# A two-layer encoder trunk on one core: where the modulated activations, their Winograd sums, the key transposes and two Fourier branch products stand

## The chip, the cores and the metric

The kernel runs on one core of a Trainium2 chip. The metric is the device time of one execution in microseconds, lower is better; the time of before is the median of three runs, 2324.62 us (2324.42 to 2328.24). Five engines matter: PE (TensorE, matrix products into PSUM), ACT (ScalarE), DVE (VectorE), POOL (GpSimd) and SP, whose queue here issues most DMAs. Each engine takes its own instructions in one fixed order.

## The reference, cut to what matters

Two groups of tokens (512 "sample" tokens and 256 "prompt" tokens, six tiles of 128 in all) pass the same DEPTH = 2 layers. What is computed per layer, with D = 1024:

```python
h = rms_norm(x, g_mix_pre) * (1 + sc1) + sh1
z = h @ w_in            # q latent 512 | kv latent 256 | rotary key 64 | Fourier input 512 | gates 2*1024
c_q, c_kv = rms_norm(z_q, g_q), rms_norm(z_kv, g_kv)
branch_a = attention(c_q @ w_q_b, c_kv @ w_kv_b, rotary parts) @ w_attn_o        # 8 heads
branch_b = fft2(u_f over sequence and 128 channels of a group).real @ w_four     # 4 groups
x = x + gt1 * rms_norm((sigmoid(gate_a) * branch_a + sigmoid(gate_b) * branch_b) @ w_out, g_mix_post)
h = rms_norm(x, g_ffn_pre) * (1 + sc2) + sh2
up = depthwise_conv3(h @ w_up)
x = x + gt2 * rms_norm((gelu(up_a) * up_b) @ w_down, g_ffn_post)
```

## The kernel before, in words

Every operand of a large product is kept as two rounded pieces, `hi` and `lo`, and a product is three matmuls: hi·hi, hi·lo, lo·hi. A piece pair costs one ACT copy (`hi`) and one DVE subtraction (`lo`); `split_from` (L195) does it from PSUM. Pools hold a fixed number of slots: 18 "doubles" (d, 128x1536), 21 "blocks" (w, 128x1024), 6 "rows" (r, 128x768), 8 PSUM banks (ps).

The work is a list of Steps. `run` walks it, and before each step it places the DMAs and the splits of weights that come due (by an estimate of PE time and the number of free blocks). The instructions of a step have a priority by their place in the list, which `tc.high_priority(offset=HP)` moves 50 forward. The framework then lays down one order for each engine: it plays the program through with its own estimates of durations and takes, whenever an engine is free, the ready instruction of the best priority, if it has a slot. On the chip that order is fixed; only waits move.

Per layer the list is, in the order of time:

- The join (end of the layer before): the last products of the feed-forward network (L1522 to L1524), per tile t the post step (L1579, L1582, mean squares on ACT L215), the residual (L684), the normalised rows (`pre_step`, L698), then h for each pair of tiles. POOL makes the reciprocal roots (L208, L211) and, at the join, the `lo` pieces of four weights (L162).
- h for a pair of tiles, the form of before at the join (`sums_h_step`): 16 transposes (L433), ACT writes a full-precision h block from PSUM (L436), ACT rounds it to `hi` (L441), DVE subtracts to `lo` (L442). For pair 1 the columns are also reversed (`reverse`, L717 on DVE and L718 on POOL). The form used for the last pair of the first layer (`h_step` with `to_h`, L374): transposes (L395), ACT writes `hi` from PSUM (L399), DVE computes `h*sc - hi` from PSUM into a row (L407) and then adds the shift, one half on DVE (L412), the other on ACT (L384), eight `hi` and eight `lo` columns a pair.
- The Fourier input products: `u_step(pair, i)`, four steps per pair of tiles and 12 matmuls a step (L802 to L804 in the second layer and for the first layer's pair 2, L1795 to L1797 for the first layer's pairs 0 and 1). `u_out` (L724 on) splits their result.
- `sums_step(pair)` (L447): four DVE additions hi + lo (L459) unless the full-precision block is at hand, four DVE differences (L471 to L477), and four splits (ACT L469, DVE L470). The result T is the moving operand of the gate products in Winograd form (`wino`, L607 to L609).
- Two plain gate products (`gate_step`, L190 to L193), 14 in Winograd form in seven `gate_pair`s, the Fourier transforms, then six key latents (`ckv_step`, L1007 to L1021, with a POOL root in each), six query latents (`cq_step`, L1034, L1036), their transposes (`kT`, `qT`, L1049 with ACT L1055 and DVE L1056), eight Fourier branch products (`four_step(m)`, 24 matmuls, two DVE multiplications L926 and L927, a POOL DMA that spills the row to DRAM, L928; the gate row comes in by an SP DMA, `load_sg`, L968), and two rotary steps (`qr`, 32 SP DMAs L1129).
- Attention (`attention`, L1148): keys and queries of a head (`k_step`, `qn_step`), rotary queries (`qr_split`, L1140), then units of scores (`sc_step`, L1229 to L1246: products, maximum, Exp, sum, scaling), transposes of the probabilities (`tr_step`, L1263) and products with V (`pv_step`).

`warm(func)` (L199) is one ACT instruction on a constant, made so that the table of `func` is loaded. Before, it stands at the end of the mixer (Exp) and of the attention (Gelu).

The order around the change:

```python
for b in range(2):
    o += [sums_step(b), gate_step(b, 7, spill(b))]
o.append(sums_step(2))
... ck[5:6], [kT(0)] + cq[0:1], [kT(1)] + cq[1:2], cq[2:3], cq[3:4], cq[4:5], [load_sg(0)] + cq[5:6],
fo[0], [qT(0)] + fo[1], [qT(1)] + fo[2], fo[3], [qr[0]] + fo[4], fo[5], [qr[1]] + fo[6], fo[7]
```

Of the kernel before, what the change touches and what calls it, by code (L numbers as in the profile page):

```python
# [48 lines left out]
def req_of(t):  # L49
    return 0 if t < 4 else 1  # L50
# [17 lines left out]
def encoder_trunk(ctx, tc, a, consts, y_prompt, y_sample):  # L68
# [29 lines left out]
    def blk(dt=F32, shape=(128, 1024)):  # L98
        blocks.append(wp.tile(list(shape), dt, tag="w", name=nm("w")))
        return blocks[-1]  # L100
# [9 lines left out]
    def bank():  # L110
        return pp.tile([128, 512], F32, tag="ps", name=nm("ps"))

    def f(ap):
        return ap.bitcast(F32)
# [81 lines left out]
        nc.scalar.activation(out=hi, in_=ps, func=AF.Copy)  # L196
        nc.vector.tensor_sub(out=lo, in0=ps, in1=f(hi))  # L197

    def warm(func):  # L199

        d = small(1)
        nc.scalar.activation(out=d, in_=neg_half, func=func)

    def rstd(sums, n=1):

# [206 lines left out]
                    nc.vector.tensor_scalar_add(out=lo[:, cols], in0=dd, scalar1=sh[:, k, r:r + 1])  # L412
        flush()

    def sums_h_step(sc, sh, pair, fold):

        r = req_of(2 * pair)

        def emit():
            if pair == 0:  # L420
                state["H"] = new_h()
            xns = [state.pop(("xn", 2 * pair)), state.pop(("xn", 2 * pair + 1))]
            c = slice(pair * 256, pair * 256 + 256)
            with tc.high_priority(offset=HP):
                h = [blk(F32, (128, 4, 2, 128)) for _ in range(2)]
                if pair == 2:
                    state["HR", pair] = h
                for i in range(4):
                    ps = bank()
                    for kk in range(2):  # L430
                        for j in range(2):
                            o = kk * 256 + j * 128
                            nc.tensor.transpose(ps[:, o:o + 128], xns[j](2 * i + kk), ident)  # L433
                    for kk in range(2):
                        k = 2 * i + kk
                        nc.scalar.activation(out=h[k // 4][:, k % 4].rearrange("p j c -> p (j c)"),  # L436
                                             in_=ps[:, kk * 256:kk * 256 + 256], func=AF.Identity,
                                             scale=state[sc][:, k, r:r + 1], bias=state[sh][:, k, r:r + 1])
                    z = h[i // 2][:, 2 * (i % 2):2 * (i % 2) + 2].rearrange("p k j c -> p k (j c)")
                    hi, lo = (x[:, :, c] for x in state["HD"][i])  # L440
                    nc.scalar.activation(out=hi, in_=z, func=AF.Copy)  # L441
                    nc.vector.tensor_sub(out=lo, in0=z, in1=f(hi))  # L442
                    if fold:
                        reverse(2 * i)
                        reverse(2 * i + 1)
        return Step(emit, 1.7)

    def sums_step(pair):

        def emit():  # L450
            if pair == 0:
                state["T"] = [(double(F32R, (128, 4, 384)), double(F32R, (128, 4, 384))) for _ in range(4)]
            h = state.pop(("HR", pair), None)
            if h is None:
                h = [blk(F32, (128, 4, 2, 128)) for _ in range(2)]
                for i in range(4):
                    hi, lo = (f(x[:, :, pair * 256:pair * 256 + 256]) for x in state["HD"][i])
                    z = h[i // 2][:, 2 * (i % 2):2 * (i % 2) + 2].rearrange("p k j c -> p k (j c)")
                    nc.vector.tensor_add(out=z, in0=hi, in1=lo)  # L459
            if pair == 2:  # L460
                del state["HD"]
            c = slice(pair * 128, pair * 128 + 128)
            r11, r12, r21, r22 = (h[kh][:, :, j, :] for kh in range(2) for j in range(2))
            t = [blk(F32, (128, 2, 4, 128)) for _ in range(2)]
            t1, t2, t3, t4 = t[0][:, 0], t[0][:, 1], t[1][:, 0], t[1][:, 1]

            def split(i, z):
                hi, lo = (x[:, :, c] for x in state["T"][i])
                nc.scalar.activation(out=hi, in_=z, func=AF.Copy)  # L469
                nc.vector.tensor_sub(out=lo, in0=z, in1=f(hi))  # L470
            nc.vector.tensor_sub(out=t1, in0=r12, in1=r11)  # L471
            split(0, t1)
            nc.vector.tensor_sub(out=t2, in0=r22, in1=t1)
            split(1, t2)
            nc.vector.tensor_sub(out=t3, in0=r22, in1=r12)
            split(2, t3)
            nc.vector.tensor_sub(out=t4, in0=r21, in1=t2)  # L477
            split(3, t4)
        return Step(emit, 0)
# [190 lines left out]
    def new_h():  # L670

        d = [(double(F32R), double(F32R)) for _ in range(4)]
        state["HD"] = [[z.rearrange("p (k c) -> p k c", k=2) for z in x] for x in d]
        return [tuple(z[:, k % 2, :] for z in state["HD"][k // 2]) for k in range(8)]
# [79 lines left out]
    def mixer_in(l, qr, fillers, start=None, tail=None):  # L754
# [54 lines left out]
            return Step(emit, 12 * 512 * MM_US, [uw[i]])  # L809

        us = [[u_step(p, i) for i in range(4)] for p in range(3)]
        out += start(uw, us, S) if start else []
        out += tail(us) if tail else []

# [148 lines left out]
        def late_mixer():  # L963

            def load_sg(m):
                def emit():
                    sgb[m] = row(F32)
                    nc.sync.dma_start(out=sgb[m], in_=gb_d[m])  # L968
                return Step(emit, 0)

            def spill(b):
                return lambda sg: nc.gpsimd.dma_start(out=(sig_d, gb_d)[b][7], in_=sg)
            o = []
            for b in range(2):
                o += [sums_step(b), gate_step(b, 7, spill(b))]
            o.append(sums_step(2))
            for m in range(7):
                st = gate_pair(m)
                if not m:
                    st = [st[i] for i in (0, 3, 1, 2, 4, 5, 6)]  # L980
                o += st[0:4] + (fill() if m else []) + st[4:]
            ck, cq = [ckv_step(t) for t in range(6)], [cq_step(t) for t in range(6)]
            fo = [[load_sg(m + 1) if m < 7 else Step(lambda: None, 0), four_step(m)] for m in range(8)]
            for x in ([dft[0], dft[1], ch[0]], [dft[2], ch[1], dft[3], ch[2]], ck[0:1], [ch[3]], ck[1:2], ck[2:3], ck[3:4],
                      ck[4:5], ck[5:6], [kT(0)] + cq[0:1], [kT(1)] + cq[1:2], cq[2:3], cq[3:4], cq[4:5], [load_sg(0)] + cq[5:6],
                      fo[0], [qT(0)] + fo[1], [qT(1)] + fo[2], fo[3], [qr[0]] + fo[4], fo[5], [qr[1]] + fo[6], fo[7]):
                o += x + fill()
            return o

# [71 lines left out]
        def kT(r):  # L1061
            def emit():
                lat_T(stage_k, 3, [vec["g_kv"][:, 0:1], vec["g_kv"][:, 1:2], None], kall, r)
                if r == 1:
                    stage_k.clear()
                    S["ckv", l], S["kr", l] = kall[0:2], kall[2]
            return Step(emit, 1.3)
# [10 lines left out]

        def end():
            S["H"] = None  # L1080
            warm(AF.Exp)
        out.append(Step(end, 0))
        return out

# [63 lines left out]
    def attention(l, qs, early):  # L1148
# [11 lines left out]
        def k_step(h):  # L1160
            w = kvw[h // 2]

            def emit():
                vh, vl = view(w, 2)
                c = slice((h % 2) * 256, (h % 2) * 256 + 128)
                p, q = bank(), bank()
                mm3_req((p, q[:, 0:256]), [(vh[:, k, c], vl[:, k, c]) for k in range(2)], S["ckv", l])
                if h % 2:
                    w.hi = w.lo = None
                hi, lo = pair()  # L1170
                split_from(p, hi[:, 0:512], lo[:, 0:512])
                split_from(q[:, 0:256], hi[:, 512:768], lo[:, 512:768])
                S["K", l][h] = (hi, lo)
            return Step(emit, 6 * 768 * MM_US, [w])

        def v_step(p, i):
# [155 lines left out]
        for u in range(n + 2):  # L1332
            if u < n:
                out.append(sc_step(u))
            if 0 <= u - 1 < n:
                out.append(tr_step(u - 1))
            out += fill[u]
            if 0 <= u - 2 < n:
                out.append(pv_step(u - 2))

        def end():
            S["ckv", l] = S["kr", l] = None
            warm(AF.Gelu_apprx_tanh)
        out.append(Step(end, 0))
        return out

# [105 lines left out]
    def ffn(l, h_last, fillers, last):  # L1452
# [203 lines left out]
                out += [ds[t] if t < NT - 1 else down_step(lc, [t], by_half=True), po[t], lo[t - 1]]  # L1656
            return out + [lo[NT - 1]]
        d45 = [down_step(lc, [4, 5], [j]) for j in range(starts[lc], NF)]
        h = [sums_h_step(("sc", l + 1, 1), ("sh", l + 1, 0), i, i == 1) for i in range(3)]
        out += [down_step(lc, [1], j1), po[1], ad[0], ad[1], pr[0], ds[2], po[2], pr[1], ad[2], ds[3], po[3], pr[2], ad[3]]  # L1660
        out += d45[0:1] + [pr[3]] + d45[1:2] + [h[0]] + d45[2:] + [po[4], po[5]]

# [249 lines left out]
```

## Time and profile before

| | before |
|---|---|
| median of 3 runs | 2324.62 us |
| the profiled execution | 2326.88 us, its span 2325.1 us |
| PE busy | 2267.4 us, 98% |
| DVE, ACT, POOL busy | 1669.4 us, 1314.4 us, 190.2 us |
| mean granted clock of PE | 0.984 |

Matmuls overlap, so a busy share counts an engine that has a matmul under way. A row of the waits says which instruction of which engine stood idle until which other one, for how long in total, how often, and the longest. A row of a timeline gives the start and duration, and in brackets the idle time of the engine just before it. A row of a stretch (A:B) gives its width, the busy time of each engine with the number of instructions, and the mean granted clock of PE, where 1.00 is the upper of its two levels, 2.4 GHz, and the other is half.

### The profile page before, as it was taken

The page shows a single profiled execution, that of the slowest core. Times are in us where ns is not written, and L with a number is a line of the kernel's source. Part 1 is how long each engine was busy: PE and PEld are TensorE (multiplying, and loading weights), DVE is VectorE, ACT ScalarE, POOL GpSimd, SP SyncE. Part 2 cuts the span into 40 slices and gives each one's busy share as a digit, 9 for nine tenths or more (in the row PEclk, how much of TensorE's full clock was granted, in tenths as well). Part 3 has the DMA queues.
Part 4 walks back from the last instruction along what each step waited for, and adds up shares of the span by engine and source line. Part 5 has one row for each costly group of instructions (what it writes and reads, how often), then busy time and mean ns, then how long its engine had stood idle before and what let it go on. Part 6 is the DMA issues. An engine that isn't in the chain of part 4 may idle for free. (4 is left out here: it accounts for less than half of the span.)

```text
span 2325.1 us, 33282 instructions
## 1 busy us (share of the span) xinstructions
PE 2267.4 (98%) x12582; PEld 2048.3 (88%) x12582; DVE 1669.4 (72%) x2712; ACT 1314.4 (57%) x2438; POOL 190.2 (8%) x317
## 2 busy tenths in 40 slices
PE   7999999999999999999989999999999999999998
PEld 5899788988899989999969988799888999999997
DVE  5976857765486887786868678677646886766677
ACT  4544516552466777777555543265425577777773
POOL 1001400000110000000130033000001000000001
PEclk9999999999989999999989999999999899999999
DMA  9356640133322433242333575302424232212223
GB/s 275 101 156 224 195 146 19 43 120 137 123 87 65 123 109 100 92 127 76 133 102 109 168 253 169 109 19 66 164 85 139 73 109 73 91 55 73 64 73 127
DMA packets 243805, 265.89 MB, mean 114 GB/s; under 512 B 20604, under 2 KB 193318, under 8 KB 243645
## 3 DMA queue, kind: packets, MB, share of 16 engines
q1 hardware_dynamic: 235885, 235.85, 32.8%
q0 software_dynamic: 7760, 27.92, 3.6%
q8 instruction: 99, 1.62, 0.3%
q14 instruction: 61, 0.50, 0.1%
HBM read 225.89 MB, written 31.54 MB: 111 GB/s over the span
## 5 line engine op out<-in xcount | busy, mean ns | idle before, releaser
L607 PE MATMUL ps<-d,w 128*128 128x384 f32 (+2 forms) x1680 | 565.2, 337 | 8.9 <-ACT ps L633 4.0
L608 PE MATMUL ps<-d,w 128*128 128x384 f32 (+2 forms) x1680 | 564.1, 336 | 0.6 <-DVE d L470 0.5
L609 PE MATMUL ps<-d,w 128*128 128x384 f32 (+2 forms) x1680 | 562.5, 335 | 0.0
L554 DVE TENSOR_TENSOR w<-w,w 128x512 fp32r<-128x512 f32 x406 | 271.6, 685 | 104.6 <-ACT w L553 101.9
L607 PEld LDWEIGHTS ps<-d,w 128*128 128x128 f32 x1680 | 322.7, 192 | 25.0 <-ACT ps L633 5.4
L608 PEld LDWEIGHTS ps<-d,w 128*128 128x128 f32 x1680 | 323.1, 192 | 10.7 <-DVE d L470 1.3
L609 PEld LDWEIGHTS ps<-d,w 128*128 128x128 f32 x1680 | 322.9, 192 | 0.9 <-DVE w L554 0.8
L553 ACT ACTIVATE w<-w 128x512 fp32r<-128x512 f32 x406 | 248.2, 626 | 71.5 <-PE ps L609 28.0
L190 PE MATMUL ps<-d,w 128*128 128x512 f32 x704 | 242.3, 345 | 0.0
L191 PE MATMUL ps<-d,w 128*128 128x512 f32 x704 | 222.2, 338 | 0.0
L161 ACT ACTIVATE w<-w 128x1024 fp32r<-128x1024 f32 (+4 forms) x140 | 141.1, 1015 | 91.9 <-PE ps L191 30.9
L319 DVE SCALAR_TENSOR_TENSOR w<-w,c,w 128x1024 f32<-128x1024 f32 x140 | 175.5, 1277 | 12.6 <-DMA w<-in_w_ada_dram 12.3
L162 DVE TENSOR_TENSOR w<-w,w 128x1024 fp32r<-128x1024 f32 (+3 forms) x136 | 157.6, 1167 | 35.7 <-ACT w L161 19.3
L193 PE MATMUL ps<-d,w 128*128 128x512 f32 x704 | 181.4, 339 | 0.0
L1560 ACT ACTIVATE w<-ps 128x512 f32<-128x512 f32 x216 | 127.4, 590 | 86.3 <-PE ps L1558 85.1
L1558 PE MATMUL ps<-w,d 128*128 128x512 f32 x432 | 171.3, 397 | 0.0
L1557 PE MATMUL ps<-w,d 128*128 128x512 f32 x432 | 170.5, 395 | 0.0
L1555 PE MATMUL ps<-w,d 128*128 128x512 f32 x432 | 167.6, 389 | 0.0
L190 PEld LDWEIGHTS ps<-d,w 128*128 128x128 f32 x704 | 132.8, 189 | 31.3 <-DVE r L926 1.7
L191 PEld LDWEIGHTS ps<-d,w 128*128 128x128 f32 x704 | 132.9, 189 | 16.2 <-DVE d L197 0.6
L1468 DVE SCALAR_TENSOR_TENSOR r<-r,v,r 128x511 f32<-128x511 f32 (+1 forms) x176 | 100.6, 613 | 33.9 <-ACT r L1465 33.6
L668 DVE TENSOR_TENSOR r<-ps,r 128x384 f32<-128x384 f32 (+2 forms) x92 | 49.3, 537 | 104.7 <-PE ps L609 104.6
(275 smaller groups left out, 4447.4 us busy)
## 6 DMA issues: line engine op xcount, KB each, us to landing
w<-in_w_up_dram SPq DMA_DIRECT2D x88, 512.0 KB, 3.9
w<-in_w_ada_dram SPq DMA_DIRECT2D x80, 512.0 KB, 3.7
w<-in_w_in_dram SPq DMA_DIRECT2D x48, 512.0 KB, 6.1
w<-in_w_down_dram SPq DMA_DIRECT2D x72, 256.0 KB, 2.9
xs<-w SPq DMA_DIRECT2D x18, 512.0 KB, 2.7
w<-xs SPq DMA_DIRECT2D x18, 512.0 KB, 3.8
w<-in_w_ada_dram SPq DMA_DIRECT2D x32, 256.0 KB, 5.8
w<-in_w_attn_o_dram SPq DMA_DIRECT2D x16, 512.0 KB, 3.6
```

The costliest lines, as they stand in the source:

```text
L190: nc.tensor.matmul(o, lh, rh[:, c0:c0 + s], start=(first and k == 0), stop=False)
L191: nc.tensor.matmul(o, lh, rl[:, c0:c0 + s], start=False, stop=False)
L193: nc.tensor.matmul(o, ll, rh[:, c0:c0 + s], start=False, stop=(last and k == n - 1))
L319: nc.vector.scalar_tensor_tensor(out=box[r], in0=x, scalar=c, in1=box[r], op0=ALU.mult, op1=ALU.add)
L553: nc.scalar.activation(out=us[i].hi, in_=z, func=AF.Copy)
L554: nc.vector.tensor_sub(out=us[i].lo, in0=z, in1=f(us[i].hi))
L607: nc.tensor.matmul(ps, wh[:, k], x, start=(start and k == 0), stop=False, skip_group_check=True)
L608: nc.tensor.matmul(ps, wh[:, k], y, start=False, stop=False, skip_group_check=True)
L609: nc.tensor.matmul(ps, wl[:, k], x, start=False, stop=(k == 3), skip_group_check=True)
L1555: nc.tensor.matmul(ps, gh[:, cc], dc.hi[:, o], start=(c == 0 and j == js[0]), stop=False, skip_group_check=True)
L1557: nc.tensor.matmul(ps, gh[:, cc], dc.lo[:, o], start=False, stop=False, skip_group_check=True)
L1558: nc.tensor.matmul(ps, gl[:, cc], dc.hi[:, o], start=False, stop=(j == js[-1]), skip_group_check=True)
```

## The change: what it does

Six edits, in both layers where not said otherwise:

1. At the join (second layer) h is made by `h_step`, the form that writes `hi` from PSUM. For pairs 0 and 1 it has the same priority as before; for pair 2 it has none. The full-precision block of pair 2 is no longer kept.
2. `sums_step(0)` stands before the last Fourier input product of pair 2, `sums_step(1)` behind it, `sums_step(2)` ahead of both plain gate products; before, each of the first two had a gate product behind it, and the third came after them.
3. `kT(0)` stands two, `kT(1)` three query latents later, `qT(0)` and `qT(1)` one Fourier product later.
4. The second rotary step stands one Fourier product earlier, and `four_step(6)` and `four_step(7)` with their `load_sg` stand in the attention, behind the score products of units 0 and 1.
5. The Exp warm-up reads a column of the first head's keys, and so follows them; it is issued in `k_step(0)`.
6. The Gelu warm-up reads a column of the last head's output.

```diff
+        us[2] = us[2][0:3] + [sums[0]] + us[2][3:] + [sums[1]]
...
-            o = []
-            for b in range(2):
-                o += [sums_step(b), gate_step(b, 7, spill(b))]
-            o.append(sums_step(2))
+            o = [sums[2]] + [gate_step(b, 7, spill(b)) for b in range(2)]
...
+            S["fo", l] = fo[6:8]
...
-                      ck[4:5], ck[5:6], [kT(0)] + cq[0:1], [kT(1)] + cq[1:2], cq[2:3], cq[3:4], cq[4:5], [load_sg(0)] + cq[5:6],
-                      fo[0], [qT(0)] + fo[1], [qT(1)] + fo[2], fo[3], [qr[0]] + fo[4], fo[5], [qr[1]] + fo[6], fo[7]):
+                      ck[4:5], ck[5:6], cq[0:1], cq[1:2], [kT(0)] + cq[2:3], cq[3:4], [kT(1)] + cq[4:5],
+                      [load_sg(0)] + cq[5:6], fo[0], fo[1], [qT(0)] + fo[2], [qT(1)] + fo[3], [qr[0]] + fo[4],
+                      [qr[1]] + fo[5]):
...
-            warm(AF.Exp)
...
+                if h == 0:
+                    warm(AF.Exp, hi[:, 0:1])
...
                 out.append(sc_step(u))
+            if u < 2:
+                out += S["fo", l][u]
...
-            warm(AF.Gelu_apprx_tanh)
+            warm(AF.Gelu_apprx_tanh, S["AT", l][NH - 1][0][:, 0:1])
...
-        h = [sums_h_step(("sc", l + 1, 1), ("sh", l + 1, 0), i, i == 1) for i in range(3)]
+        h = [h_step(("sc", l + 1, 1), ("sh", l + 1, 0), i, i == 1) for i in range(3)]
```

`sums_h_step` is removed, and `sums_step` always makes its four additions.

## Rows read from the trace of the kernel before

**Rows 1.** The page's first part: busy time, share of the span, instructions.
```profile
PE 2267.4 (98%) x12582; PEld 2048.3 (88%) x12582; DVE 1669.4 (72%) x2712; ACT 1314.4 (57%) x2438; POOL 190.2 (8%) x317
```

**Rows 2.** The waits of PE over the whole span: total us, times, longest us.
```profile
PE ps L1263 <- DVE w L1246: 8.9, 2, 4.5
PE ps L802 <- ACT d L441: 8.5, 2, 5.1
...
PE ps L179 <- DVE d L1020: 3.9, 2, 2.0
...
PE ps L607 <- ACT d L469: 3.0, 1, 3.0
...
PE ps L804 <- DVE d L442: 1.4, 1, 1.4
...
PE ps L433 <- DVE w L1579: 1.4, 1, 1.4
```

**Rows 3.** Six stretches: width, busy PE, PEld, DVE, ACT, POOL, granted clock, DMA.
```profile
88.00:108.00 20.00, 15.95 (x80) 14.66 (x79) 19.75 (x33) 11.39 (x22) 0.55 (x1) 0.91 0.34 99
236.00:262.00 26.00, 23.07 (x105) 17.27 (x104) 22.16 (x35) 10.30 (x21) 10.71 (x13) 0.93 0.58 191
340.00:366.00 26.00, 21.33 (x130) 18.67 (x130) 16.02 (x30) 13.76 (x29) 0.00 (x0) 0.93 0.25 69
1162.00:1230.00 68.00, 56.76 (x252) 45.24 (x251) 42.56 (x69) 36.27 (x76) 21.72 (x34) 0.90 0.30 93
1385.00:1411.00 26.00, 23.08 (x106) 17.31 (x105) 22.16 (x35) 10.30 (x21) 10.69 (x13) 0.93 0.60 194
1490.00:1516.00 26.00, 21.32 (x126) 18.62 (x126) 15.60 (x29) 13.73 (x28) 0.00 (x0) 0.87 0.21 59
```

**Rows 4.** Groups of DVE instructions, 62 to 108 us: busy us, mean ns, idle before.
```profile
L470 DVE TENSOR_TENSOR d<-w,d 128x512 fp32r<-128x512 f32 x12 | 7.9, 682 | 0.0
L459 DVE TENSOR_TENSOR w<-d,d 128x512 f32<-128x512 f32 x12 | 7.6, 681 | 0.0
...
L197 DVE TENSOR_TENSOR w<-ps,w 128x512 fp32r<-128x512 f32 x2 | 1.4, 686 | 2.2 <-ACT w L196 2.2
```

**Rows 5.** The stretch of one Fourier branch product, columns as in rows 3.
```profile
330.20:334.42 4.22, 4.22 (x27) 3.68 (x25) 2.19 (x4) 0.80 (x1) 0.70 (x2) 1.00 0.85 231
```

**Rows 6.** Timeline at the first attention's start: ACT table load, then DVE scaling.
```profile
350.79 1.28 ACT L1242 ACT_TABLE_LOAD   x1
...
354.23 0.87 DVE L1246 TENSOR_SCALAR w<-w,s 128x512 f32<-128x512 f32 x2
```

**Rows 7.** Rotary copies (ACT group, whole span), early warm-up (ACT), SP's rotary DMAs.
```profile
L1140 ACT ACTIVATE r<-d 128x768 fp32r<-128x768 f32 x16 | 13.5, 846 | 49.3 <-DMA d<-w 28.9 <-DMA mb_d<-r 18.0 <-PE ps L1233 2.4
...
281.57 1.28 ACT L202 ACT_TABLE_LOAD   x1
...
309.71 30.49 SPq L1129 DMA_DIRECT2D d<-w  x32
```

**Rows 8.** Timeline at the join: ACT, then DVE, then POOL.
```profile
1176.24 1.02 ACT L436 ACTIVATE w<-ps,m,m 128x256 f32<-128x256 f32 x2 [0.91 <-POOL w L162]
...
1210.07 1.06 ACT L749 ACTIVATE w<-w 128x1024 fp32r<-128x1024 f32 x1 [10.74 <-DVE w L746]
...
1159.42 0.87 DVE L698 TENSOR_SCALAR d<-w,s 128x512 f32<-128x512 f32 x2
...
1177.28 2.57 DVE L698 TENSOR_SCALAR d<-w,s 128x512 f32<-128x512 f32 x1 [4.56 <-ACT w L436]
...
1177.21 2.36 POOL L162 TENSOR_TENSOR w<-w,w 128x1024 fp32r<-128x1024 f32 x1
```

**Rows 9.** Groups of the first layer's pair 2, 54 to 63 us: ACT, DVE.
```profile
L399 ACT ACTIVATE d<-ps,m,m 128x256 fp32r<-128x256 f32 x8 | 3.9, 554 | 0.0
...
L407 DVE SCALAR_TENSOR_TENSOR r<-ps,m,d 128x256 f32<-128x256 f32 x8 | 3.7, 478 | 0.3 <-ACT d L399 0.3
L412 DVE TENSOR_SCALAR d<-r,m 128x256 fp32r<-128x256 f32 x4 | 1.4, 354 | 0.1
```

More of the change, by code (lines that the diff above doesn't have):

```diff
@@ L197, in split_from, with warm @@
         nc.vector.tensor_sub(out=lo, in0=ps, in1=f(hi))
-    def warm(func):
+    def warm(func, src=None):
         d = small(1)
-        nc.scalar.activation(out=d, in_=neg_half, func=func)
+        if src is None:
+            nc.scalar.activation(out=d, in_=neg_half, func=func)
+        else:
+            nc.scalar.activation(out=d, in_=f(src), func=func, scale=0.0)
     def rstd(sums, n=1):
@@ L413, in to_h @@
         flush()
[L415 to L446, printed above, removed]
     def sums_step(pair):
@@ L452, in emit @@
                 state["T"] = [(double(F32R, (128, 4, 384)), double(F32R, (128, 4, 384))) for _ in range(4)]
[L453 to L459, printed above, removed]
+            h = [blk(F32, (128, 4, 2, 128)) for _ in range(2)]
+            for i in range(4):
+                hi, lo = (f(x[:, :, pair * 256:pair * 256 + 256]) for x in state["HD"][i])
+                z = h[i // 2][:, 2 * (i % 2):2 * (i % 2) + 2].rearrange("p k j c -> p k (j c)")
+                nc.vector.tensor_add(out=z, in0=hi, in1=lo)
             if pair == 2:
@@ L811, in mixer_in @@
         us = [[u_step(p, i) for i in range(4)] for p in range(3)]
+        sums = [sums_step(i) for i in range(3)]
+        us[2] = us[2][0:3] + [sums[0]] + us[2][3:] + [sums[1]]
         out += start(uw, us, S) if start else []
```

## The prediction

> **What bounds the kernel now.** I read the busy times first: PE is busy 98% of the span, the next engine 72% [rows 1]. So time can come only from stretches in which PE stands still or runs at its lower clock, and an edit that takes work off another engine is worth nothing by itself. The second view is the list of PE's waits [rows 2]; the reader is to see how short it is, and that nearly all of it lies in six places: the sums of the first layer (L607, 3.0 us), the key transposes in both layers (L179, 3.9 us), the first transposes of probabilities in both layers (L1263, 8.9 us) and the join (L802, L804, L433: 8.5 + 1.4 + 1.4 us). The third view gives each place a stretch of its own, with PE's idle time and the granted clock [rows 3]. A wait is followed by a stay at 1.2 GHz, where the products take twice as long, so a place loses its idle time plus its busy time times (1 - clock):
>
> sums, first layer: 4.05 + 15.95 x 0.09 = 5.5 us; key transposes: 2.93 + 23.07 x 0.07 = 4.5 and, in the second layer, 4.5; attention's start: 4.67 + 21.33 x 0.07 = 6.2 and 4.68 + 21.32 x 0.13 = 7.5; join: 11.24 + 56.76 x 0.10 = 16.9. In all 45.1 us.
>
> The edits leave PE's products as they are, so 45.1 us is also about the most that they can gain. The question is what share of it comes back.
>
> **The change, part by part.**
>
> *The sums (edit 2).* A sums step is 12 DVE instructions of 128x512 at 0.68 us, some 0.6 us from start to start, and 4 ACT copies: 7.3 us of DVE, 22 us for three. In the first layer DVE is the late one there: 19.75 of 20 us busy while PE waits, with 2.2 us of idle time ahead of the first sums [rows 3, 4]. The move lets the first sums fill these 2.2 us, and puts the third ahead of the weight pieces (L554) that are made for later gate products; by an estimate six of these, at 0.68 us each as every instruction of this shape, stand ahead of the wait and can come after it. Together that is 2.2 + 4.1 us against a wait of 3.0 and its clock. Bounds: 0 (the weight pieces then are late instead) and 5.5. I take 4.0, since DVE has little to spare. In the second layer no wait of PE stands at the sums, so nothing is gained: 0. Cover for both: the last input product and two plain gate products, in which PE needs no sum.
>
> *Key transposes (edit 3).* In the key latents ACT stands on POOL's roots, the transposes then wait, and their PSUM banks hold up the next query latent; the wait is put down to L1020, one of the last DVE instructions of a key latent [rows 2]. With two and three query latents between, the chain is done when the transposes come. Nothing reads the keys before attention; the three tiles of key latents are only held longer. Bounds for a layer: 0 (the banks merely run out later, behind the same DVE work) and 4.5. I take 3.8, so 7.6 for both. The query transposes then have one Fourier product of 4.2 us [rows 5] ahead of the rotary step as cover, in place of two; if that is too short, a wait of a microsecond takes its place, which is in the 0.7 left.
>
> *Fourier products in attention, and the Exp table (edits 4 and 5).* At the start of attention PE has two score products and one key product, and then waits 4.5 us in each layer for the scaled probabilities (L1246). On the way lie a table load of 1.28 us and copies ahead of it on ACT [rows 2, 6]. The Exp warm-up of before had loaded at 281.57, 70 us early [rows 7]; the Gelu one behind it replaced the table, and the load fell into the chain. Two products of 4.2 us each [rows 5] now lie between the first scores and these transposes: 8.4 us of cover for 4.5, and either one nearly covers it alone; with the early table the chain is shorter by 1.28 besides. The new warm-up waits for a copy that stands ahead of it on ACT anyway; behind it stands the first query's copy, which comes only after a product as long as the two here. The products bring four DVE multiplications, 2.2 us [rows 5], on an engine with 16.0 of 26 us busy [rows 3], two spills by POOL, behind which nothing waits, and one SP load. SP is occupied by the rotary copies for 30.5 us up to 340.2 [rows 7]; the last of them are issued 4.2 us earlier now, as the second rotary step is, so the load is there in time. Bounds: 0 and 13.7. I take 12.5.
>
> *The Gelu warm-up (edit 6).* It takes a load away that no wait of PE stands behind: 0; the end of attention bears one load of 1.28 us on ACT, where PE has other products.
>
> *h at the join (edit 1).* For pair 0 ACT started at 1176.24, when POOL's weight piece had let go a block [rows 8]. The new form needs no block, so ACT can start when the transposes are done, before the last down products end, and the waits of 3.4 (8.5 - 5.1) and 1.4 us go. But pair 1 stays as late as it was: its last row is scaled from 1177.28 on and takes 2.57 us instead of the 0.4 of its like, beside a POOL weight piece of 2.36 us [rows 8]; its transposes stand in PE's fixed order among the products of pair 0, so I put 2 us of waiting there. For pair 2 ACT stood 10.7 us before a copy of `u_out` (L749), with h of pair 2 behind it [rows 8], and PE waited 5.1 us. Without its priority the transposes now come after the products of pair 1: ACT takes `hi` at once, but `lo` stands behind four DVE additions of `u_out` (2.7 us), so 2.6 us stay. The bank wait of 1.4 stays too. Price: a pair costs DVE 8 x 0.478 + 4 x 0.354 = 5.2 us [rows 9] against 4 x 0.68 = 2.7 before; three pairs and the additions that pair 2 now needs (2.7) make 10.2 us more, in a stretch with 25 idle DVE us of 68 [rows 3]. Left over: 2.0 + 2.6 + 1.4, and 2.5 for two stays at the lower clock, together 8.5. Gain 16.9 - 8.5 = 8.4. Bounds: -5 (half of the 10.2 us exposed) and 16.9.
>
> The row that speaks against this price is that 2.57: a DVE instruction from SBUF alone was held for as long as POOL's piece ran [rows 8]. By the Trainium skill ("SBUF — State Buffer", section "SBUF: two separate sides") VectorE and GpSimd take a shared port pair in turn, each for a whole instruction, and a VectorE operation in the two-port mode is shut out until GpSimd's ends. By that rule, with which the row agrees, `to_h`'s additions from SBUF (L412) could each wait a whole piece, 2.4 us, beside POOL's last two, and the join would give 3.6 instead of 8.4, 2297 in all.
>
> **Sum.** 4.0 + 7.6 + 12.5 + 8.4 = 32.5 us. From the profiled execution's own 2326.9 that gives 2294.4; the median of the runs shown is 2.3 us below it, so I predict 2292.
>
> **The rivals.**
>
> *The join gives nothing.* Pair 1's rows come no earlier, and PE's queue holds transposes that wait for them; beside POOL's last two pieces two of the additions L412 take 2.57 us instead of 0.35 (4.4 us), and 4 of DVE's 10.2 us more stand open. For it: all behind 1177 us hangs on a DVE instruction beside POOL [rows 8]. Against: pair 0 was late for a block alone, and pair 2 for an ACT order that ends. 2292 + 8.4 = 2300.
>
> *ACT stands on a row in attention.* The rotary copies (L1140) waited 18.0 us for spills of Fourier products, about 9 us in each layer [rows 7], as six rows are all. The last two spills now come later, and the first Exps may stand behind such a copy. Then the transposes come 8.9 - 1.3 us later, against 8.4 us of cover for what was a wait of 4.5: 3.7 us and 1.5 at the lower clock stay in each layer, and the 12.5 shrinks to 3.3: 2301.
>
> *The change doesn't do what it says.* The orders are laid down by estimates; they can put the transposes ahead of the products and the additions behind the weight pieces, as the Exp warm-up came 70 us early [rows 7]. All places keep their waits: 2324.
>
> *Slower: the products of the join lose their overlap.* If DVE works off the early sums (14.6 us for two) ahead of a pair's `lo`, each pair's h stands bare before its products: three times some 7 us by ACT's and DVE's rows [rows 9], 21 us, and between such waits all 144 products stay at 1.2 GHz, 512 x 144 columns at 4.22 us for 9,216 [rows 5], so 33.8 us more. The join loses 54.8 instead of 16.9, the rest gains 24.1: 2324.6 + 37.9 - 24.1 = 2338. It decides from a loss of 41 us at the join. Against: h of pairs 0 and 1 has priority, and a clock below 0.90 over 68 us is in no row.
>
> **How the numbers follow.** The forecast's case, 2284 to 2299, gets 0.55; the join without gain 0.18; the rows in attention 0.13; no effect 0.06; slower 0.08. The runs can tell 0.2% (4.6 us) from no change. Faster by more than that: the first three, 0.86. Within: 0.06. Slower: 0.08. The range goes from 2278, just under the 2279.5 at which all 45.1 us come back, to 2315, where each place gives little (1 + 2 + 6 + 0 us). It leaves out the last two cases, 0.14.
>
> **What would show it.** Right: L607 without a wait for L469 near 95 us; no L179 wait for L1020; no L1263 wait above 1 us, an ACT table load behind the first key copies and two warm loads fewer a layer; products of pair 0 right behind the last down products at the join, waits of 2 to 3 us for pairs 1 and 2. Wrong: PE waits on L926's banks or on L1140 in attention, L609's weights late at the first gate pair, a granted clock below 0.90 at the join, or a wait of over 5 us before pair 1 there.

## The result, and the profile after

The changed kernel takes 2294.65 us (median of 4 runs, 2293.9 to 2299.15) where the kernel before takes 2326.43 (4 runs beside it): a ratio of 0.9867, 95% interval 0.985 to 0.9885. Its profiled execution took 2294.44 us with a span of 2292.6, so the spans differ by 32.5 us; the sum of the prediction was 32.5. The time forecast was 2292: it took 2.3 us off because the three runs of before then known had their median below the profiled one, and with the fourth that median is 2326.43.

Where they come from is read best from the starts of PE's products, since both kernels do the same products. *Start* ends at the first input product (L802, now L770). A goes from the first gate pair of the first layer to its first Fourier transform, B from there to the last transposes of probabilities. C goes from the first down unit of the first layer to the first gate pair of the second, so it holds the join. D and E are A and B of the second layer. In us, worked out from the traces:

```
         start      A       B       C       D       E
before   61.24  110.39  309.32  544.18  105.09  309.80
after    59.85  106.92  299.88  537.13  104.37  299.84
gain      1.39    3.47    9.44    7.05    0.72    9.96
e1                              544.40  103.38
e2                      304.10                  304.15
e3              110.93                  112.78
e4                      304.07                  303.85
e5                      300.96                  301.25
e6                              535.31
e7                              527.87
e8                              532.98
e9                              532.98
e10                     302.67                  303.52
e11                     306.25                  305.85
e12             111.76          537.24          309.60
```

The experiments' rows (below) show only the stages that they bear on. Each row comes from one profiled execution. Where a stage has no edit, B and E differ by about 0.4 us at most between runs, C by 0.7, D by 1.2, A by up to 1.4 (before against e12). *Start* went from 59.23 to 62.40 over all runs with no edit in it, so its 1.4 us are not the change's; the experiments are compared by their stages first, by their medians second; the two differ by 3.4 us at most (e10).

The waits of PE after, over the whole span (total us, times, longest), to be held against [rows 2]:

```profile
PE ps L770 <- DVE r L410: 5.0, 1, 5.0
PE ps L575 <- ACT ps L601: 4.5, 6, 1.1
...
PE ps L180 <- DVE w L162: 2.0, 2, 1.0
PE ps L398 <- DVE w L1551: 1.4, 1, 1.4
```

The waits of the sums, of L179 and of L1263 (now L1233) are gone; the second row was there before with 4.0 us. One long wait is new: five microseconds at the join, behind an instruction that the prediction does not name. The stretches that answer to [rows 3], with the same columns, each aligned to the same work:

```profile
86.00:106.00 20.00, 18.57 (x103) 17.16 (x102) 18.72 (x32) 12.91 (x25) 1.09 (x2) 1.00 0.35 99
236.00:262.00 26.00, 24.99 (x122) 19.71 (x121) 24.18 (x32) 11.07 (x22) 6.65 (x10) 1.00 0.75 214
328.00:354.00 26.00, 25.11 (x153) 21.66 (x152) 20.97 (x37) 14.93 (x31) 1.17 (x2) 1.00 0.29 94
1145.00:1213.00 68.00, 60.97 (x288) 49.97 (x287) 57.94 (x110) 39.39 (x82) 27.63 (x36) 0.95 0.33 105
1370.00:1396.00 26.00, 24.99 (x120) 19.65 (x119) 24.09 (x32) 10.62 (x22) 6.73 (x10) 1.00 0.64 191
1458.00:1484.00 26.00, 25.11 (x153) 21.68 (x152) 20.07 (x35) 13.67 (x30) 1.18 (x2) 1.00 0.34 107
```

Five of the six now run at 1.00 throughout, with about 1 us of idle time each. The join keeps 7.03 us of idle time and a clock of 0.95: 7.03 + 60.97 x 0.05 = 10.1 us of its 16.9 are still lost. DVE, POOL, ACT and PE there (start, duration, in brackets the idle time before; in this order):

```profile
1146.07 3.59 DVE L652 SCALAR_TENSOR_TENSOR w<-d,s,w 128x512 f32<-128x512 f32 x2 [0.45 <-POOL s L214]
...
1152.90 3.06 DVE L666 TENSOR_SCALAR d<-w,s 128x512 f32<-128x512 f32 x2 [0.84 <-POOL s L214]
...
1162.41 2.55 DVE L666 TENSOR_SCALAR d<-w,s 128x512 f32<-128x512 f32 x1 [3.55 <-POOL s L214]
1164.89 0.86 DVE L410 SCALAR_TENSOR_TENSOR r<-ps,m,d 128x256 f32<-128x256 f32 x2
...
1146.05 2.40 POOL L162 TENSOR_TENSOR w<-w,w 128x1024 fp32r<-128x1024 f32 x1
...
1152.83 2.39 POOL L162 TENSOR_TENSOR w<-w,w 128x1024 fp32r<-128x1024 f32 x1
...
1158.94 2.40 POOL L162 TENSOR_TENSOR w<-w,w 128x1024 fp32r<-128x1024 f32 x1 [2.57 <-PE ps L1496]
1161.44 0.30 POOL L211 TENSOR_SCALAR s<-s 128x1 f32<-128x1 f32 x1
...
1162.35 2.34 POOL L162 TENSOR_TENSOR w<-w,w 128x1024 fp32r<-128x1024 f32 x1
...
1159.74 0.19 ACT L218 ACTIVATION_READ_ACCUMULATOR d<-w 128x1 f32 x1
...
1165.90 0.77 PE L770 MATMUL ps<-w,d 128*128 128x512 f32 x1 [4.99 <-DVE r L410]
1167.34 2.79 PE L398 MATMUL ps<-ident,d 128*128 128x128 f32 x12 [0.67 <-DVE r L410]
```

Pair 0's products start at 1160.07, right behind the last down products, and stop after three of them: the fourth waits 5.0 us, and pair 1's transposes (L398) behind it another 0.7. The fourth waits for L410, whose output no product reads: so it must be waiting for a PSUM bank of pair 0's transposes, which L410 has still to read. L410 stands behind L666 of row 3 in DVE's order; L666 waits 3.55 us for POOL's root, which stands behind a weight piece (row 3's mean square on ACT ends at 1159.93, the root L211 starts at 1161.44, so 1.5 us of it); and then L666 runs beside the next piece and takes 2.55 us. That is the reading; e6 to e9 test it. (Line numbers differ a little from kernel to kernel.)

### The profile page after: what moved, and what is told of

Same layout as the page of the kernel before. It is cut to its first block, busy times and chain, and to the rows that moved or that the text cites. A ratio compares the mean times of both kernels' runs of the same rounds, so it can differ in the third digit from the quotient of the medians.

```text
span 2292.6 us, 33289 instructions
## 1 busy us (share of the span) xinstructions
PE 2252.8 (98%) x12582; PEld 2037.7 (89%) x12582; DVE 1676.0 (73%) x2740; ACT 1306.9 (57%) x2434; POOL 187.4 (8%) x317
## 5 line engine op out<-in xcount | busy, mean ns | idle before, releaser
L162 DVE TENSOR_TENSOR w<-w,w 128x1024 fp32r<-128x1024 f32 (+3 forms) x136 | 158.0, 1168 | 31.7 <-ACT w L161 15.1
```

## The experiments

**Undoing one part.** *e1*: `h = [sums_h_step(...)]` at the join in place of `h_step`, with the kept block.

> The changed kernel, but with h at the join made as before: ACT writes a full-precision block, then hi and lo come from it, with priority for all three pairs, and the third sums step uses the kept block. The other five edits stay. Theory A (each edit has its own stretch, and the gains add): the stretch from the first product of the final down projection to the first gate pair of the second layer is 7.0 us longer, 2301.7 in all; PE waits again for h of pair 0 (3 to 5 us) and of pair 2. Theory B (the join got faster because the sums of the second layer moved, not because of the new h): no more than 2 us, 2296.5. Theory C (the early sums take DVE from the old h of pair 2, which the priority does not prevent for instructions already under way): more than 9 us, 2304 or above.

2300.57 us (0.9889, 0.9876 to 0.9903). C is 544.40, 7.27 longer than after and as long as before, with the waits of before:

```profile
PE ps L805 <- ACT d L444: 8.5, 2, 5.1
PE ps L807 <- DVE d L445: 1.4, 1, 1.4
```

Theory A for the place and the size: with the sums where the change puts them, the old h brings back the whole loss. That h alone was the cause does not follow (e7).

*e2*:
```diff
-cq[0:1], cq[1:2], [kT(0)] + cq[2:3], cq[3:4], [kT(1)] + cq[4:5],
+[kT(0)] + cq[0:1], [kT(1)] + cq[1:2], cq[2:3], cq[3:4], cq[4:5],
```

> The changed kernel, but with the two key transposes behind the first and second query latent as before; the query transposes and all else as changed. Theory A (the transposes waited for the chain of the last key latent, and two query latents are enough cover): the waits of L179 for the key chain come back, 3.5 us in each layer with the stay at the lower clock, 2301.7. Theory B (the banks run out behind the same DVE work wherever the transposes stand): within 2 us of the changed kernel.

2300.23 us (0.9889, 0.9876 to 0.9903); B and E are 4.2 and 4.3 longer, and the wait of [rows 2] is back to the tenth of a microsecond. Theory A. By medians the loss is 5.6 us and not 8.5: the profiled execution, 2302.5 us, was the longest of the four.

```profile
PE ps L179 <- DVE d L989: 3.9, 2, 2.0
```

*e3*:
```diff
-us[2] = us[2][0:3] + [sums[0]] + us[2][3:] + [sums[1]]
-o = [sums[2]] + [gate_step(b, 7, spill(b)) for b in range(2)]
+o = [sums[0], gate_step(0, 7, spill(0)), sums[1], gate_step(1, 7, spill(1)), sums[2]]
```

> The changed kernel, but with the sums steps at their old places between and behind the two plain gate products, in both layers. Theory A: the first layer loses 3.5 us, with PE waiting about 3 us for the third sums' copies; the second layer loses 0 to 0.7; 2298.5 in all. Theory B (in the second layer the early sums stand in DVE's queue against h of pair 2 and cost there what they give): the second layer gains 1 to 2 us, so 2296.5.

2307.58 us (0.9918, 0.9905 to 0.9932), far from either theory. A is 4.0 longer, as A said; D is 8.4 longer. The wait for the sums' copies, and the 20 us from the first gate pair of the second layer on:

```profile
PE ps L575 <- ACT d L437: 8.2, 2, 5.3
```
```profile
1226.00:1246.00 20.00, 13.80 (x67) 12.38 (x66) 19.93 (x33) 12.31 (x23) 0.54 (x1) 0.83 0.28 81
```

DVE is busy 19.93 of 20 us: this reads as the backlog of the new h, which costs DVE more and leaves the sums of pair 2 four additions that the old h's kept block had spared. D for the four cases: old h and old places 105.09 (before), old h and early sums 103.38 (e1), new h and old places 112.78, new h and early sums 104.37 (after). The gains don't add: in the second layer edit 2 mostly pays what edit 1 costs.

*e4*: all eight `fo` in the mixer, none behind the scores.

> The changed kernel, but with all eight Fourier branch products ahead of attention as before; the Exp table is still loaded behind the first key copies. Theory A (the two products of 4.2 us are the cover): PE waits 3 us in each layer for the scaled probabilities, 1.28 us less than before because the table is loaded, and with the stay at the lower clock the kernel loses 4 to 5 us in each layer: 2303.5. Theory B (the table load and the copies behind it were what mattered): less than 1.5 us in each layer, 2297.

2304.0 us (0.9904, 0.989 to 0.9917); B and E 4.2 and 4.0 longer. Theory A: it gave a wait of 3 us a layer, and 3.2 are there:

```profile
PE ps L1232 <- DVE w L1215: 6.3, 2, 3.2
```

*e5*: `warm(AF.Exp)` and `warm(AF.Gelu_apprx_tanh)` at their old places.

> The changed kernel, but with the Exp and Gelu warm-ups at their old places, reading a constant; the two Fourier branch products stay in attention. Theory A (two products of 4.2 us are more cover than the chain of 4.5 us with its table load needs): no wait above 1 us comes back, within 1 us of the changed kernel, 2294.5. Theory B (the load of 1.28 us in the chain is not covered, because the key copies follow the products): 1.3 to 2 us more in each layer, 2297.5.

2299.16 us (0.9896, 0.9876 to 0.9916); B and E 1.1 and 1.4 longer. By size between the theories, nearer to B: the cover was not ample. PE's wait for the scaling is back with 1.8 us a layer, behind this order on ACT:

```profile
PE ps L1232 <- DVE w L1215: 3.6, 2, 1.8
```
```profile
336.40 0.85 ACT L1109 ACTIVATE r<-d 128x768 fp32r<-128x768 f32 x1
...
338.09 0.84 ACT L1109 ACTIVATE r<-d 128x768 fp32r<-128x768 f32 x1
...
340.41 1.28 ACT L1211 ACT_TABLE_LOAD   x1
341.70 0.69 ACT L1211 ACTIVATE w<-ps,s 128x512 f32<-128x512 f32 x1
```

Beside the load two rotary copies (L1109) stand ahead of the first Exp. In the changed kernel the Exp starts at 337.26, behind the same key copies (L196) but before the rotary copy (L1108). So e5 does not measure the table load alone. It also puts back both warm-ups: Gelu's again loads right behind Exp's (277.65 behind 272.73), so the two edits are not told apart. In the changed kernel the table was loaded behind the first key copies:

```profile
316.98 0.87 ACT L196 ACTIVATE d<-ps 128x512 fp32r<-128x512 f32 x2 [6.68 <-PE ps L193]
317.87 1.28 ACT L205 ACT_TABLE_LOAD   x1
```

**How much cover.** *e10* and *e11* leave one product in attention and put the other back as the mixer's last (`S["fo", l] = [[], fo[7]]` and `[fo[7], []]`).

> The changed kernel, but only one Fourier branch product stands in attention, behind the scores of unit 1; the other is back ahead of attention. Theory A (the chain of first Exps begins with the copies behind the key product, so the product behind unit 1 is the whole cover, 4.2 us for 3.2): the same time as the changed kernel within 1 us, no wait above 1 us at the first transposes. Theory B (both products are needed): 1.5 to 4 us in each layer, 2298 to 2302.

> As e10, but the one product stands behind the scores of unit 0. Theory A (it lies ahead of the key product whose copies start the chain, so it covers nothing): PE waits 3 us a layer at the first transposes as without any product in attention, 8.5 us slower than the changed kernel, 2303. Theory B (either one covers the chain nearly alone): within 2 us of the changed kernel, 2296.

e10: 2304.48 us (0.9905, 0.9892 to 0.9917), B and E 2.8 and 3.7 longer; theory B by its stages, while the median lies beyond its 2302 (*start*, 2.5 us longer in the profiled execution, is part of that). The transposes wait, and ahead of them DVE:

```profile
PE ps L1233 <- DVE w L1216: 4.8, 2, 2.4
```
```profile
342.30 0.69 DVE L896 TENSOR_TENSOR r<-ps,r 128x512 f32<-128x512 f32 x1 [3.95 <-PE ps L193]
...
344.04 1.88 DVE L197 TENSOR_TENSOR w<-ps,w 128x512 fp32r<-128x512 f32 x3
...
346.49 0.87 DVE L1216 TENSOR_SCALAR w<-w,s 128x512 f32<-128x512 f32 x2
```

DVE stands 3.95 us for the product's own multiplication (L896), with the key's `lo` and the scaling queued behind it; in the changed kernel L1216 starts at 339.17 and the second L896 at 343.40. What is meant as cover for PE is here a wait on DVE. e11: 2308.12 us (0.9921, 0.9909 to 0.9932), B and E 6.4 and 6.0 longer, worse than with no product at all (e4). Theory A's place, and more than its size: the product stands ahead of the key product whose copies start the chain, so it covers nothing, and in this order a rotary copy stands in the chain besides. From the first key copy to the first Exp ACT takes 4.24 us (339.38 to 343.62), in e4 3.14 (337.61 to 340.75), and PE's wait is longer by the same 1.1 us. That is the prediction's second rival on a small scale.

```profile
PE ps L1233 <- DVE w L1216: 8.6, 2, 4.3
```
```profile
341.44 0.85 ACT L1108 ACTIVATE r<-d 128x768 fp32r<-128x768 f32 x1 [0.24 <-issue]
```

**The join's remainder.** *e6*: `+ [h[0]] + [pr[3]] + d45[2:]`, row 3 laid down behind h of pair 0.

> The changed kernel, but at the join the scaling of row 3 (L666) is laid down behind h of pair 0 instead of ahead of it. In the changed kernel PE stops after three products of pair 0 for 5.2 us, then 1.2 us, and starts pair 1's transposes 7.3 us after the last down product. Theory A (DVE works in order: the scaling of row 3, which waits for POOL behind a weight piece, holds pair 0's second half and with it a PSUM bank): no product of pair 0 waits for L410, and only pair 1's transposes wait for row 3, 4 to 5 us; 1.5 to 2.5 us faster than the changed kernel, 2292.5. Theory B (the wait is for row 3 whatever DVE does first): the same time, the wait now at the transposes with 6 us or more, 2294.5.

2293.99 us (0.9874, 0.9858 to 0.989); C 1.8 shorter, theory A's size; the medians, 0.7 us apart, don't tell the two kernels apart. The place is clear: no product of pair 0 waits above 0.2 us, and pair 1's transposes wait 2.9 + 1.5. But L415, an addition from SBUF that elsewhere takes 0.34 us, now stands beside the pieces (POOL 1159.57 to 1161.97 and 1163.73 to 1166.13) and ends 0.15 us after each:

```profile
1161.22 0.90 DVE L415 TENSOR_SCALAR d<-r,m 128x256 fp32r<-128x256 f32 x1
...
1163.84 0.87 DVE L410 SCALAR_TENSOR_TENSOR r<-ps,m,d 128x256 f32<-128x256 f32 x2
1164.63 1.65 DVE L415 TENSOR_SCALAR d<-r,m 128x256 fp32r<-128x256 f32 x1
```

*e8*: e6, and h of pair 1 without priority.

> The changed kernel with two edits at the join: the scaling of row 3 behind h of pair 0, and h of pair 1 without priority, so that its transposes are spread among the last products of pair 0 instead of standing behind the first three. Theory A (the stop after three products is nothing but the order, and 12 products of pair 0 and more can run while row 3 is scaled): the stop of 6.4 us goes, no wait above 1.5 us takes its place, and the stays at the lower clock go with it (the stretch of 68 us shows 0.98 or more): 6 to 8.5 us faster than the changed kernel, 2287. Theory B (pair 1's h then comes late for the products of pair 1, since its reversed copies stand behind two rows on DVE): a wait of 3 to 6 us ahead of pair 1, 2292 to 2295.

2291.91 us (0.9863, 0.9847 to 0.9879); C 4.15 shorter, between the theories. The clock over 1145 to 1213 is 1.00 and no wait is above 1.5 us, as A said, but three waits stay, the first of them ahead of pair 1, where B put it:

```profile
PE ps L770 <- DVE w L685: 1.5, 1, 1.5
PE ps L398 <- DVE w L1551: 1.4, 1, 1.4
PE ps L398 <- DVE r L410: 1.1, 1, 1.1
```

*e7*: `w.eng = nc.vector` for the join's four pieces, nothing else.

> The changed kernel, but the lower halves of the four weight pieces of the join are made by DVE instead of POOL (four instructions of 1.17 us more on DVE, four of 2.4 us fewer on POOL). Theory A (POOL's pieces hold its roots for row 3 and slow the DVE instruction beside them): the scaling of row 3 takes 0.9 us for both halves and comes 2 us earlier or more, PE's stop after three products of pair 0 shrinks from 6.4 to 3 us or less, 2291. Theory B (DVE is the bound of the join, and 4.7 us more on it come out at PE): 2 to 5 us slower than the changed kernel, 2297.

2287.03 us (0.9841, 0.9825 to 0.9858), the fastest of all; C 9.3 shorter, more than theory A said. It has more work on DVE and less waiting:

```profile
1145.00:1213.00 68.00, 67.13 (x340) 56.08 (x339) 65.08 (x130) 44.55 (x94) 17.35 (x33) 1.00 0.37 115
```
```profile
1147.64 1.42 DVE L652 SCALAR_TENSOR_TENSOR w<-d,s,w 128x512 f32<-128x512 f32 x2 [0.45 <-POOL s L214]
...
1157.86 0.88 DVE L666 TENSOR_SCALAR d<-w,s 128x512 f32<-128x512 f32 x2
```

DVE is busy 65 of 68 us, PE idle for 0.87 at a full clock. L652 takes 1.42 instead of 3.59, L666 0.88 instead of 3.06. The 1.4 us bank wait, which the prediction left standing, went too.

*e9* tells apart the two ways in which a piece can cost: by roots queued behind it on POOL, or by holding DVE.

```diff
             (w.eng or nc.vector).tensor_sub(out=o_(w.lo), in0=i_(w.raw), in1=f(o_(w.hi)))
+            if w.twice:
+                nc.gpsimd.tensor_sub(out=blk(F32)[:, 0:w.n], in0=i_(w.raw), in1=f(o_(w.hi)))
```

> The kernel of e7 (all four pieces of the join on DVE), and in addition POOL makes the lower halves of the third and fourth piece once more into a block that nobody reads. All four roots of rows 2 and 3 stand ahead of these two in POOL's queue and the next root comes some 8 us later, so nothing waits for POOL. Theory P (POOL's piece holds DVE instructions beside it whose operands all lie in SBUF, for as long as it runs): two DVE instructions take about 2.2 us longer than their like, and since DVE has hardly any idle time in this stretch PE loses 2 to 4.5 us against e7: 2290. Theory Q (POOL's pieces cost only because roots stand behind them in its queue): the same time as e7, 2287, and no DVE instruction is longer.

2291.59 us (0.9849, 0.9836 to 0.9862); C 5.1 longer than in e7. PE waits 4.4 us, and two DVE instructions are long (DVE, then POOL; L417 and L412 are the L415 and L410 of the other kernels):

```profile
1157.41 1.21 DVE L162 TENSOR_TENSOR w<-w,w 128x1024 fp32r<-128x1024 f32 x1
...
1159.33 1.72 DVE L417 TENSOR_SCALAR d<-r,m 128x256 fp32r<-128x256 f32 x1
1160.96 3.35 DVE L162 TENSOR_TENSOR w<-w,w 128x1024 fp32r<-128x1024 f32 x1
...
1165.03 0.34 DVE L417 TENSOR_SCALAR d<-r,m 128x256 fp32r<-128x256 f32 x1
...
1156.69 6.54 POOL L164 TENSOR_TENSOR w<-w,w 128x1024 f32<-128x1024 f32 x2 [0.24 <-DVE d L417]
```

Theory P: nothing waits for POOL's repeats, yet DVE loses 1.72 - 0.34 and 3.35 - 1.21, 3.5 us, and PE's wait grows by as much (0.9 us in e7). Two repeats cost 5.1 us of C, about half of what four real pieces cost (9.3), so the holding alone can account for their price; what the roots queued behind them add was not measured by itself.

*e12*: e7's edit in the kernel before.

> The kernel before, with one edit: the lower halves of the four weight pieces of the join are made by DVE instead of POOL. Theory A (POOL's pieces were behind most of the join's loss, the late block of pair 0 and the long scaling of row 3): the join's 16.9 us fall to 5 or less, 10 to 14 us faster than the kernel before, though h is made the old way: 0.9945. Theory B (the old h itself sets the join: ACT's block, its priority and the order behind u_out): at most 5 us faster, 0.998.

2320.68 us (0.9975, 0.9965 to 0.9985); C 6.9 shorter than before. Between the theories, nearer to B: ACT's order still keeps its wait of 5.1 us.

```profile
PE ps L802 <- ACT d L441: 5.1, 1, 5.1
```

C of the four: old h with POOL's pieces 544.2, old h without 537.2, new h with 537.1, new h without 527.9. Either edit alone gives 7, both give 16.3 of the 16.9 that the prediction put as the most.

## Why the prediction was right, and where not

*What bounds the kernel* held: PE's waits and the stays at 1.2 GHz behind them account for the result, and by the same reckoning the six stretches stopped losing 29.8 us of the 32.5.

*The sums*: 4.0 predicted, 3.5 in this pair of traces and 4.0 in e3, in a stage that varies by up to 1.4. The price "in the second layer: 0" is right only for both edits together; the text costed edit 2 by PE's waits before and did not ask what edit 1 would do to DVE there (e3: 8.4 us).

*Key transposes*: 7.6 predicted, 8.5 measured by e2's stages (5.6 by its medians). Cover for the query transposes sufficed: no wait of theirs is among PE's waits after.

*Attention*: 12.5 predicted, 10.9 measured (B and E less e2's share); e4 gives 8.2 for the products, and e5 2.5 for the table load (1.28) together with the rotary copies that its order puts ahead of the Exps. The step that failed is "either one nearly covers it alone". It set 4.2 us against 4.5 on PE alone. e10 shows that a product in PE's queue also has instructions in DVE's, which can hold the chain that it should cover (2.4 us of waiting left); e11 shows that a product ahead of the key product covers nothing (4.3 us left). By the traces the pair works because the scaling stands ahead of the second product's multiplications on DVE; no run tests that order by itself. ACT's rotary copies, the second rival, did not stop the changed kernel; in e5 and e11 they stand in the chain.

*The join*: 8.4 predicted, 7.05 measured, and the parts are not those predicted. Pair 0's own waits (3.4 and 1.4) went, as said. "Pair 1's transposes, 2 us" was 5.0 + 0.7, through DVE's order and a PSUM bank in place of PE's order: a wait of over 5 us before pair 1 was one of the prediction's own signs of being wrong, and it came. "Pair 2, 2.6 us" was nothing that shows: PE is busy without a break from 1170 to 1213, where products of the gate fill the gap. DVE instructions are held beside POOL's pieces (L652 3.59 us for 1.42, L666 3.06 for 0.88), which the prediction weighed at a price of 4.8 us. The rule of the Trainium skill ("SBUF — State Buffer", section "SBUF: two separate sides") also names VectorE operations with two SBUF inputs, against a GpSimd operation that reads SBUF. The traces agree: L652 and, in e9, L162 have two such inputs and were held 2.2 and 2.1 us. The prediction's place was off: not L412 (now L415) but L652 and L666 are held in the changed kernel, and in the kernel before too, where I read one such row (2.57) and left the join's gain to h. The trace of before has two more, beside the pieces at 1160.73 and 1167.51, which I passed over:

```profile
1160.74 3.59 DVE L684 SCALAR_TENSOR_TENSOR w<-d,s,w 128x512 f32<-128x512 f32 x2 [0.45 <-POOL s L211]
...
1167.58 3.01 DVE L698 TENSOR_SCALAR d<-w,s 128x512 f32<-128x512 f32 x2 [0.85 <-POOL s L211]
```

*The Gelu warm-up*: no wait shows for it, but it was undone only together with the Exp warm-up (e5), so its own worth is not shown. There are six table loads in all instead of ten.

That the total agrees to a tenth is luck: the start (1.4, in no step), D (0.7, no more than its spread between runs), keys (0.9) and 0.4 in the stages between made up for the sums (0.5), attention (1.6) and the join (1.4).

## What to carry to other kernels

An elementwise piece that is given to POOL "because DVE is busy" can cost DVE its whole length; look for DVE instructions of one form with two durations, and which POOL row lies beside the long one. A product moved in as cover for PE brings its reader into another engine's in-order queue, so its place there has to be read as well. And edits that meet on one engine cannot be priced apart: undone one at a time (e1 to e5, by their stages) the five lose 7.3 + 8.5 + 12.4 + 8.2 + 2.5 = 38.9 us of a whole of 32.5.

## What was not expected of the hardware

DVE instructions with all operands in SBUF that began while POOL's 128x1024 subtraction (2.4 us) was at work were 0.6 to 2.2 us longer than their like (L652, L666, L415, L162). Those that read PSUM (L410 in e6: 0.88 and 0.87 for two with a piece at work, 0.87 without) were not. It can go the other way as well: in e9 DVE's L162 at 1157.41 kept its 1.21 us beside the first repeat, which began at 1156.69 beside another DVE instruction from SBUF, and of POOL's two subtractions, 6.54 us together, the first took 4.20 us and the second 2.37 (POOL's own spans are rough).
